# Softmax units before stick-breaking units, and the diff branch's w_o products moved beneath the latter, in a two-layer attention trunk

## The chip, the cores and the metric

The kernel runs on one core of a Trainium2 chip. The metric is the device time of one execution in microseconds, as the median of several runs. The engines are TensorE (PE, matmuls and transposes), VectorE (DVE), ScalarE (ACT), GpSimd (POOL) and SyncE (SP, which issues most of the transfers). TensorE's clock has two levels, 2.4 and 1.2 GHz; the profile gives the granted clock as a share of the higher one.

## What is computed

Two layers run over a sequence of 512 rows of width 1024, in float32. Each is an attention part and a SwiGLU FFN (hidden width 2816); a last RMS norm ends the trunk. Of the attention part:

```python
h = rms_norm(x, g_attn)
proj = h @ w_in            # diff q,k,v; stick-breaking q,k,v; 2 x 1024 gate columns
dq, dk = apply_rope(dq), apply_rope(dk)
w = softmax(dq1 @ dk1) - lam * softmax(dq2 @ dk2)      # 4 diff heads, causal
o_diff = rms_norm(w @ dv, subln) * (1 - lam_init)
log_beta, log_rem = log_sigmoid(z), log_sigmoid(-z)    # z = sq @ sk / 8, 8 stick-breaking heads
a = exp(log_beta + cumsum_from_the_right(log_rem))
o_sb = a @ sv
g_diff, g_sb = split(sigmoid(gates + b_gate))
merged = g_diff * (o_diff @ w_o_diff) + g_sb * (o_sb @ w_o_sb)
x = x + merged @ w_out
```

## The kernel before

Everything lies transposed, features on the 128 partitions and the 512 rows along the free axis. A float32 operand is held as two parts, `hi` (rounded) and `lo` (the rest), and each product of a 128 x 128 tile is three matmuls, `hi.hi`, `lo.hi`, `hi.lo` (`mm_tiles`, L254). A projection to 128 columns from all 1024 features ("a group") is thus 8 x 3 = 24 matmuls of 128x512.

Weights are streamed in the order in which they are used: SP loads a tile into `wr`, ACT rounds it to `wh` (L127), and DVE, or POOL for every fourth tile of `w_in`, makes `wl` = `wr` - `wh` (L128-L129). Four tiles of `wh` and `wl` exist, and a tile is prepared two groups ahead.

PSUM has eight banks: three with the tag `mm` (projections) and five with `at` (scores, transposes, attention products).

In the attention part of a layer, eight units follow one another. Each has three groups (k, q, v) and two maps of scores:
- Four stick-breaking units (SB, names with `s`), first in the order. A map is scores (L465), two sigmoids on ACT (L504, L506), a scan on DVE (L509), a product on POOL (L511), ten transposes (L488) which ACT and DVE copy out as `ths` and `tls` (L491, L492), and a product with v, `avs` (L522, L523).
- Four softmax units (Diff, names with `d`). Their k and q are rotated in `rope` (L400): ACT copies the projection to `us`, POOL multiplies it by the sine table `cs[:,1]` (L405), DVE by the cosine table (L406), four DMAs on SP swap blocks of 32 partitions (L409), and POOL adds (L410). The tables `cs` are multiplied by the norm factor `r` once in each layer (L355, L356). Exponentials stand on ACT (L551), the division by the first map's sums on POOL (L559), the mix of the two maps on DVE (L567). The output is normed per head: three ACT passes over the product `avd` (`ofd`, `osd`, `ohd`, L582 to L587), a mean by PE (`omd`, L589), then logarithm and exponential on ACT (L206, L207) and steps on DVE.

After its k is made (`stack_k`, L428), a unit's casts are `ka`, `kb` on ACT and DVE. The value group (`value`, L447) is first scaled by `r` on DVE (L397), then transposed on PE (`vt`, L450).

The layer's norm factor `r` comes from a matmul (`msa`, L246), logarithm and exponential on ACT and three DVE steps (L205 to L211). Unit 0's three groups are computed ahead of it, on `at` banks; the groups of unit 1 follow.

A loop of 18 steps (L614) puts the work in program order: the first half of map i, groups from a list `slots`, the second half of map i - 2. `slots` names for each unit the groups that stand beside it: the three of the next unit, and gate groups (16 in all), so that the first four units have 3 groups each, the last four 4. Nine gate groups remain for the end. Then come the splitting of the eight outputs into parts (L636), and for each of eight column tiles m of w_o two products, `ws` (stick-breaking half) and `wd` (diff half), whose gates get their sigmoid there (L655) and are multiplied and summed on DVE. ACT holds one table of functions at a time; explicit loads stand at L341 (sigmoids), L623 (logarithm and exponential) and L666. Within these dependences a list scheduler puts each engine's instructions in order when the program is built; each engine runs its list in order and waits where an operand is missing.

Of the kernel before, what the change touches and what calls it, by code (L numbers as in the profile page):

```python
# [8 lines left out]
F32 = mybir.dt.float32  # L9
# [25 lines left out]
BUFS = dict(mx=4, sm=4, blk=12, tmp=5, stk=6, v=3, wk=4, wT=3)  # L35
BANK_BUFS = dict(mm=3, at=5)
W_BUFS, W_AHEAD = 4, 2
GATES_IN_BLK = 4
# [6 lines left out]
FILL = (3, 3, 3, 3, 4, 4, 4, 4)  # L45
# [8 lines left out]
def trunk(ctx: ExitStack, tc, xT, par, tab, scn, msk, w_in, w_o, w_out, w_fi, w_fo, out):  # L54
# [11 lines left out]
    UNITS = [("s", i) for i in range(4)] + [("d", i) for i in range(4)]  # L66
# [5 lines left out]
    GATES = []  # L72
    for m in range(8):
        GATES += [("in", 24 + 8 + m), ("in", 24 + m)]
    layer_order = list(unit_groups(UNITS[0]))
    slots = []
    gi = 0
    for n in range(8):
        g = unit_groups(UNITS[n + 1]) if n < 7 else []
        while len(g) < FILL[n] and gi < len(GATES):  # L80
            g.append(GATES[gi])
            gi += 1
        slots.append(g)
# [18 lines left out]
    def w_src(k):  # L102
        l, kind, i = k[:3]
        if kind == "fo":
            c0, c1 = CHUNKS[k[3]]
            return w_fo[l, i][:, c0 * P:c1 * P]
        return {"in": w_in, "o": w_o, "out": w_out, "fi": w_fi}[kind][l, i]
# [4 lines left out]
    def w_pieces(*steps):  # L112
# [10 lines left out]
        for n_cols in steps:  # L123
# [4 lines left out]
            eng = nc.gpsimd if stream[n][1] == "in" and n % 4 == 0 else nc.vector  # L128
# [199 lines left out]
    for l in range(DEPTH):  # L328
        h = nrm.h
        with ExitStack() as ac:  # L330
# [10 lines left out]
            table("sigmoid_and_others", state["exp"])  # L341
# [4 lines left out]

            def blk(name, dt=F32):
                return T("blk", name, dt=dt)
# [6 lines left out]
            nc.vector.tensor_tensor(out=cs[:, 0], in0=cs[:, 0], in1=r, op=ALU.mult)  # L355
            nc.vector.tensor_tensor(out=cs[:, 1], in0=cs[:, 1], in1=r, op=ALU.mult)  # L356
# [8 lines left out]
            pair = [None]  # L365
            TAIL = list(TAIL0)

            def gate_group(key):
# [3 lines left out]
                n = len(gates)  # L372
                if n < GATES_IN_BLK:
                    t = blk(f"gt{j}")
                elif n < GATES_IN_BLK + BUFS["stk"]:
                    t = T("stk", f"gt{j}")
                elif n < GATES_IN_BLK + BUFS["stk"] + 2:
                    t = T(f"klz0{n - GATES_IN_BLK - BUFS['stk']}", f"gt{j}")
                else:
                    q = (n - GATES_IN_BLK - BUFS["stk"]) % 2  # L380
                    if q == 0:
                        pair[0] = T("wk", f"gt{j}", (P, 1280))
                    t = pair[0][:, q * S:q * S + S]
# [112 lines left out]
            class SB(Unit):  # L496
                def maps(self, c):
# [5 lines left out]
                    for i, (o, n) in enumerate(BANKS):  # L503
                        nc.scalar.activation(out=e[:, o:o + n], in_=bs[i][:, :n], func=AF.Sigmoid, scale=-0.125)  # L504
                    for i, (o, n) in enumerate(BANKS):
                        state["sig"] = nc.scalar.activation(out=z[:, o:o + n], in_=bs[i][:, :n], func=AF.Sigmoid,  # L506
                                                            scale=0.125)

                    nc.vector.tensor_tensor_scan(out=e[:, ::-1], data0=e[:, ::-1], data1=msc[:, ::-1], initial=1.0,  # L509
                                                 op0=ALU.mult, op1=ALU.max)  # L510
# [3 lines left out]
                def mix(self, c, a):  # L514
# [9 lines left out]
                    if c == 0:  # L524
                        self.o = blk("o" + self.n)
# [11 lines left out]
            class Diff(Unit):  # L537
                def maps(self, c):
# [75 lines left out]
            for i in range(16 + LAG):  # L614
# [5 lines left out]
                if i < 16:  # L620
                    units[i // 2].first(i % 2)
                    if i == 7:
                        state["tab"] = table(LNEXP, state["sig"])  # L623
# [281 lines left out]
```

## Time and profile before

| | |
|---|---|
| runs | 1496.0, 1497.68, 1497.97 us (median 1497.68) |
| profiled execution | 1496.57 us, span 1494.8 us, granted clock 0.995 |
| PE busy | 1461.4 us, 98% of the span |
| DVE busy | 976.0 us, 65% |
| ACT busy | 691.8 us, 46% |
| POOL busy | 483.0 us, 32% |
| transfers | 139.73 MB, 93 GB/s on average |

The time of an execution is its span and 1.8 us around it. Busy shares are means over stages: stick-breaking units stand from about 40 to 140 us and 775 to 880 us, softmax units from 140 to 230 and 880 to 970 us, and the rest are gate, w_o, w_out and FFN products. The windows give each engine's busy time stage by stage. The end of a matmul is modelled by the profile, so a pause behind one looks shorter than from start to start.

### The profile page before, as it was taken

What the parts mean: (1) busy time and instruction counts of PE and PEld (TensorE: products, weight loads), DVE (VectorE), ACT (ScalarE), POOL (GpSimd) and SP (SyncE); (2) the same over time, 40 slices, a digit from 0 to 9 for tenths busy, and PEclk for the clock granted to TensorE, in tenths of its full rate; (3) what the DMA queues carried; (4) which work ended last, traced back from release to release, by engine and by line L of the source; (5) the groups of instructions that cost most, each with busy time, mean ns of one, the idle gap of its engine ahead of it and who ended that gap; (6) DMA issues with size and microseconds to landing.
All of it is one profiled execution on the core that took longest, in us unless ns stands there. A gap on an engine that the chain in (4) does not pass through costs nothing.

```text
span 1494.8 us, 19780 instructions
## 1 busy us (share of the span) xinstructions
PE 1461.4 (98%) x7670; PEld 1253.0 (84%) x7670; DVE 976.0 (65%) x1229; ACT 691.8 (46%) x1122; POOL 483.0 (32%) x317
## 2 busy tenths in 40 slices
PE   9899999999999999999998999999999999999996
PEld 7788888888888998998886878888888989989885
DVE  6978776475765757654658777765648467477544
ACT  5656554643642433433444645546336334335342
POOL 2454652001140723530224455510022226155112
PEclk9999999999999999999999999999999999999998
DMA  7122232132323323223421122322323233232232
GB/s 254 46 78 69 75 102 86 57 124 94 106 96 103 108 87 105 90 83 87 134 85 57 64 75 88 100 81 80 103 94 117 90 99 113 74 124 71 87 88 66
DMA packets 45934, 139.73 MB, mean 93 GB/s; under 512 B 5904, under 2 KB 8336, under 8 KB 45840
## 3 DMA queue, kind: packets, MB, share of 16 engines
q1 hardware_dynamic: 45120, 137.91, 28.7%
q8 instruction: 60, 0.98, 0.3%
q10 hardware_dynamic: 720, 0.56, 0.1%
q14 instruction: 34, 0.28, 0.1%
HBM read 132.16 MB, written 2.10 MB: 90 GB/s over the span
## 4 chain that ended last, share of the span: by engine, by line
PE 87%; DVE 6%; ACT 3%; issue 1%; POOL 1%; DMA 1%; SPq 0%; DVEq 0%; POOLq 0%; ACTq 0%
PE fa L725 8%; PE fc L725 4%; PE pg L259 4%; PE pg L260 4%; PE pg L261 4%; PE fo L259 3%; PE fo L260 3%; PE fo L261 3%; PE fg L259 3%; PE fg L260 3%; PE fu L261 3%; PE fg L261 3%; PE fu L260 3%; PE fu L259 3%; PE fb L725 2%; PE wo L259 2%
## 5 line engine op out<-in xcount | busy, mean ns | idle before, releaser
L127 ACT CAST wh<-wr 128x1024 fp32r<-128x1024 f32 (+4 forms) x223 | 213.8, 964 | 327.5 <-issue 55.3
L129 DVE TENSOR_TENSOR wl<-wr,wh 128x1024 fp32r<-128x1024 f32 (+3 forms) x201 | 247.6, 1236 | 77.4 <-ACT wh L127 75.9
L259 PE MATMUL pg<-hha,wh 128*128 128x512 f32 x256 | 101.0, 394 | 0.0
L261 PE MATMUL pg<-hla,wh 128*128 128x512 f32 x256 | 100.3, 392 | 0.0
L260 PE MATMUL pg<-hha,wl 128*128 128x512 f32 x256 | 100.1, 391 | 0.0
L129 POOL TENSOR_TENSOR wl<-wr,wh 128x1024 fp32r<-128x1024 f32 (+3 forms) x22 | 50.7, 2305 | 111.8 <-ACT wh L127 99.2
L706 POOL TENSOR_TENSOR p<-u,g 128x512 f32<-128x512 f32 x22 | 34.4, 1563 | 158.0 <-DVE u L763 154.5
L242 POOL TENSOR_TENSOR accf<-accf,sqf 128x512 f32<-128x512 f32 x10 | 18.5, 1846 | 199.9 <-ACT sqf L240 199.9
L259 PE MATMUL fo<-ah,wh 128*128 128x512 f32 (+1 forms) x220 | 82.8, 376 | 0.0
L260 PE MATMUL fo<-ah,wl 128*128 128x512 f32 (+1 forms) x220 | 82.6, 375 | 0.0
L261 PE MATMUL fo<-al,wh 128*128 128x512 f32 (+1 forms) x220 | 82.3, 376 | 0.0
L259 PE MATMUL pd<-hha,wh 128*128 128x512 f32 x192 | 76.4, 398 | 0.3 <-ACT knd3s L404 0.3
L260 PE MATMUL pd<-hha,wl 128*128 128x512 f32 x192 | 76.2, 397 | 0.0
L261 PE MATMUL pd<-hla,wh 128*128 128x512 f32 x192 | 76.0, 396 | 0.0
L144 POOL TENSOR_TENSOR tf<-ru,rg 128x512 f32<-128x512 f32 x22 | 31.8, 1446 | 128.5 <-DMA ru<-in_w_fi_dram 112.3
L259 PE MATMUL fg<-hhf,wh 128*128 128x512 f32 x176 | 69.1, 393 | 0.0
L260 PE MATMUL fg<-hhf,wl 128*128 128x512 f32 x176 | 69.1, 393 | 0.0
L261 PE MATMUL fu<-hlf,wh 128*128 128x512 f32 x176 | 68.7, 390 | 0.0
L261 PE MATMUL fg<-hlf,wh 128*128 128x512 f32 x176 | 68.7, 390 | 0.0
L260 PE MATMUL fu<-hhf,wl 128*128 128x512 f32 x176 | 68.6, 390 | 0.0
L259 PE MATMUL fu<-hhf,wh 128*128 128x512 f32 x176 | 68.6, 390 | 0.0
L259 PE MATMUL ps<-hha,wh 128*128 128x512 f32 x144 | 58.8, 409 | 0.0
(452 smaller groups left out, 4492.0 us busy)
## 6 DMA issues: line engine op xcount, KB each, us to landing
wr<-in_w_in_dram SPq DMA_DIRECT2D x78, 512.0 KB, 3.3
wr<-in_w_fi_dram SPq DMA_DIRECT2D x44, 512.0 KB, 3.3
wr<-in_w_fo_dram SPq DMA_DIRECT2D x32, 384.0 KB, 3.1
rg<-in_w_fi_dram SPq DMA_DIRECT2D x22, 512.0 KB, 3.3
ru<-in_w_fi_dram SPq DMA_DIRECT2D x22, 512.0 KB, 3.3
wr<-in_w_fo_dram SPq DMA_DIRECT2D x32, 320.0 KB, 2.9
wr<-in_w_o_dram SPq DMA_DIRECT2D x16, 512.0 KB, 3.3
wr<-in_w_out_dram SPq DMA_DIRECT2D x16, 512.0 KB, 3.3
```

The costliest lines, as they stand in the source:

```text
L127: nc.scalar.copy(out=hi[:, c], in_=raw[:, c])
L129: state["wl"] = eng.tensor_tensor(out=lo[:, c], in0=raw[:, c], in1=f32(hi[:, c]), op=ALU.subtract)
L144: tt = lambda eng, o, a, b: eng.tensor_tensor(out=o, in0=a, in1=b, op=ALU.subtract)
L242: eng.tensor_tensor(out=self.acc, in0=self.acc, in1=sq, op=ALU.add)
L259: nc.tensor.matmul(dst, hi[:, c], rh, start=first and k == 0, stop=False)
L260: nc.tensor.matmul(dst, lo[:, c], rh, start=False, stop=False)
L261: nc.tensor.matmul(dst, hi[:, c], rl, start=False, stop=last and k == n - 1)
L706: (nc.vector if u.space == bass.MemoryType.PSUM else nc.gpsimd).tensor_tensor(out=p, in0=u, in1=g, op=ALU.mult)
L725: nc.tensor.matmul(dst, x[:, c], y, start=first and k + n == 0, stop=n == 2 and k == len(a) - 1, skip_group_check=True)
```

## The change

The softmax units come first and the stick-breaking units last. `slots` is written out: one gate group of the diff half beside each of the first three units, two beside the fourth and the fifth, then the last one. w_o is loaded in halves of 512 columns. The diff halves (`od`, 12 matmuls each) become fillers beside the stick-breaking units: each product is multiplied into its gate as soon as it is there (`od_group`); so the diff outputs are split into parts inside `mix`. The stick-breaking halves (`os`) are left for the end, the first two of them with three of their four units early. Five gate groups remain for the end. One load of the sigmoid table stands behind the last softmax unit's exponentials; the gates made so far get their sigmoid there and the later ones as they come; the load of the logarithm's table stands behind the last of them. The loads at the start of a layer and amid the units go. POOL makes no `wl` of a layer's first seven tiles. Gates and outputs get buffers of their own, and the scratch for DMA descriptors is halved. The matmuls are the same in number and size, DMA issues go from 358 to 374 (halves), ACT_TABLE_LOADs from 13 to 9.

```diff
-    UNITS = [("s", i) for i in range(4)] + [("d", i) for i in range(4)]
+    UNITS = [("d", i) for i in range(4)] + [("s", i) for i in range(4)]
...
+    GD, GS = [("in", 24 + m) for m in range(8)], [("in", 32 + m) for m in range(8)]
+    OD = [("od", m) for m in range(8)]
+    slots = [GD[0:1], GD[1:2], GD[2:3], GD[3:5], GD[5:7], GD[7:8] + OD[0:2], OD[2:6], OD[6:8] + GS[0:3]]
+    for n in range(7):
+        slots[n] = unit_groups(UNITS[n + 1]) + slots[n]
+    TAIL0 = GS[3:8]
...
+        if kind in ("od", "os"):
+            return w_o[l, i][:, 512 * (kind == "os"):][:, :512]
...
-            eng = nc.gpsimd if stream[n][1] == "in" and n % 4 == 0 else nc.vector
+            eng = nc.gpsimd if stream[n][1] == "in" and n % 4 == 0 and n % len(layer_order) > 6 else nc.vector
...
             r = nrm.finish()
-            table("sigmoid_and_others", state["exp"])
...
+            def od_group(m):
+                b = bank("mm", f"wd{m}_{l}")
+                hi, lo = w_get(l, "od", m)
+                mm_tiles(b, hi, lo, od_, True, True)
+                nc.vector.tensor_tensor(out=gates[m], in0=b, in1=gates[m], op=ALU.mult)
...
+            def sigmoid(j):
+                bias = pt[:, C_BG + 16 * l + j:C_BG + 16 * l + j + 1]
+                with tc.issue_after(state["tab"].ins):
+                    sigs.append(nc.scalar.activation(out=gates[j], in_=gates[j], func=AF.Sigmoid, bias=bias))
...
+                    od_.append(parts(o, T("osp", "oh" + self.n, dt=F32R), T("osp", "ol" + self.n, dt=F32R)))
...
+                    if i == 8:
+                        fill(g.pop(0))
+                        units[3].second(1)
+                        state["tab"] = table("sigmoid_and_others", state["exp"])
+                        for j in sorted(gates):
+                            sigmoid(j)
                     units[i // 2].first(i % 2)
-                    if i == 7:
-                        state["tab"] = table(LNEXP, state["sig"])
...
-                bs, bd = fbank(f"ws{m}_{l}"), fbank(f"wd{m}_{l}")
-                mm_tiles(bs, hi, lo, os_, True, True, 4)
-                mm_tiles(bd, hi, lo, od_, True, True, 0)
+                if m < 2:
+                    b, hi, lo = ws[m]
+                    mm_tiles(b, hi, lo, os_[3:], False, True, 3)
+                else:
+                    b = fbank(f"ws{m}_{l}")
+                    mm(b, (l, "os", m), os_)
...
-            table(LNEXP, sig)
+            with ExitStack() as order:
+                for s in sigs[:-1]:
+                    order.enter_context(tc.issue_after(s.ins))
+                table(LNEXP, sigs[-1])
```

How the built order of three engines moves. First DVE at the start of layer 0, behind the norm factor `ya0`; `p00` to `p02` are unit 0's k, q and v groups. Before:

```order
L355 TENSOR_TENSOR cs_0_322<-cs_0_322,ya0_311 128x512
L356 TENSOR_TENSOR cs_0_322<-cs_0_322,ya0_311 128x512
L397 TENSOR_TENSOR kns0_0_334<-p00_0_197,ya0_311 128x512
L397 TENSOR_TENSOR qns0_0_344<-p01_0_198,ya0_311 128x512
L397 TENSOR_TENSOR vns0_0_352<-p02_0_199,ya0_311 128x512
L397 TENSOR_TENSOR kns1_0_420<-ps10_0_389,ya0_311 128x512
L397 TENSOR_TENSOR qns1_0_461<-ps11_0_430,ya0_311 128x512
L433 CAST kas0_0_336<-kns0_0_334 64x512
L434 CAST kbs0_0_337<-kns0_0_334 64x512
```

and now:

```order
L206 SCALAR_TENSOR_TENSOR ya0_311<-ta0_312,ya0_311 128x512
L348 TENSOR_TENSOR cs_0_321<-cs_0_321,ya0_311 128x512 x2
L408 TENSOR_TENSOR knd0_0_334<-knd0s_0_335,cs_0_321 128x512
L125 TENSOR_TENSOR wl9_647<-wr9_645,wh9_646 128x1024
L408 TENSOR_TENSOR qnd0_0_353<-qnd0s_0_354,cs_0_321 128x512
L435 CAST kad0_0_344<-knd0_0_334 64x512
L436 CAST kbd0_0_345<-knd0_0_334 64x512
L399 TENSOR_TENSOR vnd0_0_369<-p02_0_199,ya0_311 128x512
L437 TENSOR_TENSOR klz00_0_325<-knd0_0_334,kad0_0_344 64x512
L438 TENSOR_TENSOR klz01_0_326<-knd0_0_334,kbd0_0_345 64x512
L457 TENSOR_TENSOR vd0_0_376<-vtd0_0_371,vd0_0_376 128x512
```

The scaling of the value group, the fifth operation behind the factor before, now stands behind both table products, two cosine products, a weight subtraction and the two casts of the rotated k (`knd0`). On PE the transpose that reads it stands at the same place in both, behind the groups of unit 1.

Second PE at the end of softmax unit 1 in layer 0 (the product is `avd1`, the mean `omd1`, gate group 26 `pg26`, the scores of unit 3 `sd30`). Before:

```order
L260 MATMUL pg26_0_2275<-hha06_161,wl29_2183 128x512
L261 MATMUL pg26_0_2275<-hla06_162,wh29_2182 128x512
L259 MATMUL pg26_0_2275<-hha07_166,wh29_2182 128x512
L260 MATMUL pg26_0_2275<-hha07_166,wl29_2183 128x512
L261 MATMUL pg26_0_2275<-hla07_167,wh29_2182 128x512
L589 MATMUL omd1_0_2100<-ohd1_0_2101,ones_v_79 128x512
L473 MATMUL sd300_0_2148<-kad3_0_1931,qad3_0_1981 128x128
```

and now:

```order
L576 MATMUL avd1_0_1131<-thd1_0_1113,vd1_0_576 128x256
L577 MATMUL avd1_0_1131<-tld1_0_1114,vd1_0_576 128x256
L578 MATMUL avd1_0_1131<-thd1_0_1113,vd1_0_576 128x256
L576 MATMUL avd1_0_1131<-thd1_0_1113,vd1_0_576 128x128
L577 MATMUL avd1_0_1131<-tld1_0_1114,vd1_0_576 128x128
L578 MATMUL avd1_0_1131<-thd1_0_1113,vd1_0_576 128x128
L588 MATMUL omd1_0_1148<-ohd1_0_1149,ones_v_79 128x512
L475 MATMUL sd300_0_1200<-kad3_0_980,qad3_0_1030 128x128
L476 MATMUL sd300_0_1200<-klz10_0_327,qad3_0_1030 128x128
```

Before, a whole gate group of 24 matmuls stands between the product (further up) and the mean; now the mean follows the product's last matmul.

Third ACT at the start of layer 0, where `wh8` is the ninth weight tile, whose other part POOL makes. Before:

```order
L127 CAST wh7_496<-wr7_495 128x1024
L206 ACTIVATE ya0_311<-msa0_309,eps_81 128x512
L207 ACTIVATE ya0_311<-ya0_311 128x512
L268 ACT_TABLE_LOAD
L127 CAST wh8_564<-wr8_563 128x1024
L127 CAST wh9_638<-wr9_637 128x1024
```

and now:

```order
L123 CAST wh7_540<-wr7_539 128x1024
L123 CAST wh8_581<-wr8_580 128x1024
L202 ACTIVATE ya0_311<-msa0_309,eps_81 128x512
L203 ACTIVATE ya0_311<-ya0_311 128x512
L406 COPY qnd0s_0_354<-p01_0_198 128x512
L123 CAST wh9_646<-wr9_645 128x1024
L433 CAST kad0_0_344<-knd0_0_334 64x512
L434 CAST kbd0_0_345<-knd0_0_334 64x512
```

The cast of the ninth tile has moved ahead of the logarithm of the norm, and the table load between is gone.

## Rows read from the trace of the kernel before

**Rows 1.** Windows: us, busy by engine (x instructions), PEclk, DMA share, GB/s.

```profile
40.00:80.00 40.00, 32.84 (x160) 26.85 (x159) 36.99 (x35) 22.65 (x42) 20.49 (x10) 0.96 0.16 53
80.00:140.00 60.00, 58.46 (x318) 49.33 (x317) 46.55 (x48) 38.62 (x72) 32.11 (x16) 1.00 0.22 71
140.00:280.00 140.00, 139.70 (x707) 118.56 (x707) 96.85 (x156) 68.30 (x144) 60.10 (x40) 1.00 0.28 87
...
780.00:820.00 40.00, 32.94 (x161) 26.57 (x160) 31.97 (x23) 20.17 (x41) 21.75 (x9) 0.96 0.13 42
820.00:880.00 60.00, 57.38 (x310) 48.66 (x309) 45.96 (x51) 35.97 (x67) 26.79 (x15) 1.00 0.21 69
```

**Rows 2.** Waits of PE: what for, us in total, times, longest.

```profile
PE avs L523 <- DVE tls L492: 10.0, 7, 3.8
PE vts L450 <- DVE vns L397: 3.1, 1, 3.1
...
PE avs L522 <- ACT ths L491: 1.4, 2, 1.1
```

**Rows 3.** Windows behind the long waits; PEclk is third from the end.

```profile
46.00:48.00 2.00, 2.00 (x6) 1.51 (x6) 1.97 (x2) 1.19 (x3) 1.79 (x2) 0.50 0.00 0
48.00:50.00 2.00, 2.00 (x8) 1.59 (x7) 1.97 (x3) 0.00 (x0) 0.00 (x0) 0.67 0.00 0
...
806.00:808.00 2.00, 1.39 (x7) 1.39 (x8) 1.48 (x3) 0.48 (x1) 0.00 (x0) 0.77 0.80 260
808.00:810.00 2.00, 2.00 (x7) 1.61 (x7) 0.00 (x0) 1.95 (x5) 1.65 (x2) 0.50 0.01 2
```

**Rows 4.** Timeline of PE, layer 1: start us, us, instruction, [idle before <- releaser].

```profile
759.94 0.40 PE L260 MATMUL ps<-hha,wl 128*128 128x512 f32 x1
...
771.97 0.39 PE L259 MATMUL ps<-hha,wh 128*128 128x512 f32 x1
```

**Rows 5.** Timeline of PE, start of layer 0.

```profile
40.86 0.39 PE L261 MATMUL ps<-hla,wh 128*128 128x512 f32 x1
44.34 0.66 PE L450 MATMUL vts<-ident,vns 128*128 128x128 f32 x4 [3.09 <-DVE vns L397]
```

**Rows 6.** Timeline of DVE, start of layer 0.

```profile
39.61 2.87 DVE L356 TENSOR_TENSOR cs<-cs,ya 128x512 f32<-128x512 f32 x1
...
43.60 0.68 DVE L397 TENSOR_TENSOR vns<-p,ya 128x512 f32<-128x512 f32 x1
...
48.18 1.22 DVE L129 TENSOR_TENSOR wl<-wr,wh 128x1024 fp32r<-128x1024 f32 x1
```

**Rows 7.** Timeline of POOL, start of layer 0.

```profile
39.18 2.76 POOL L129 TENSOR_TENSOR wl<-wr,wh 128x1024 fp32r<-128x1024 f32 x1 [12.81 <-ACT wh L127]
```

**Rows 8.** Lines 405, 410, 433, 434: ns min/median/max, first and last start.

```profile
L405 POOL TENSOR_TENSOR knd0u<-knd0s,cs x2: 1315/1524/1732, 106.0 to 846.2; 128x512 f32<-128x512 f32 x2
...
L410 POOL TENSOR_TENSOR knd<-knd,knd0s x2: 1294/1713/2132, 112.0 to 852.0; 128x512 f32<-128x512 f32 x2
...
L433 DVE CAST kad<-knd x8: 420/421/2668, 114.2 to 958.9; 64x512 fp32r<-64x512 f32 x8
...
L434 DVE CAST kbs<-kns x8: 422/423/2565, 46.8 to 822.7; 64x512 fp32r<-64x512 f32 x8
```

**Rows 9.** Timeline of POOL, first rope of layer 1.

```profile
852.04 1.29 POOL L410 TENSOR_TENSOR knd<-knd,knd0s 128x512 f32<-128x512 f32 x1 [4.07 <-DMA knd0s<-knd0u]
```

**Rows 10.** Timeline of POOL, start of layer 1.

```profile
766.60 2.41 POOL L129 TENSOR_TENSOR wl<-wr,wh 128x1024 fp32r<-128x1024 f32 x1 [17.92 <-ACT wh L127]
```

**Rows 11.** Timeline of ACT, end of the first softmax unit of layer 0.

```profile
198.21 0.59 ACT L582 COPY ofd<-avd 128x512 f32<-128x512 f32 x1 [0.81 <-PE avd L578]
...
199.18 0.61 ACT L587 ACTIVATE ohd<-avd 128x512 fp32r<-128x512 f32 x1
```

**Rows 12.** Timeline of ACT, table load at the start of layer 0.

```profile
36.75 1.28 ACT L268 ACT_TABLE_LOAD   x1
38.05 1.05 ACT L127 CAST wh<-wr 128x1024 fp32r<-128x1024 f32 x1
```

More of the change, by code (lines that the diff above doesn't have):

```diff
@@ L44 @@
 H = S // 2
-FILL = (3, 3, 3, 3, 4, 4, 4, 4)
 LAG = 2
@@ L70, in unit_groups @@
         return [("in", c + i) for c in ((4, 0, 8) if kind == "d" else (16, 12, 20))]
-    GATES = []
-    for m in range(8):
-        GATES += [("in", 24 + 8 + m), ("in", 24 + m)]
-    layer_order = list(unit_groups(UNITS[0]))
[L76 to L83, printed above, removed]
+    GD, GS = [("in", 24 + m) for m in range(8)], [("in", 32 + m) for m in range(8)]
[4 more added lines that the diff above has]
+    TAIL0 = GS[3:8]
+    layer_order = list(unit_groups(UNITS[0]))
+    for g in slots + [TAIL0]:
         layer_order += g
-    TAIL0 = GATES[gi:]
-    layer_order += TAIL0
-    layer_order += [("o", m) for m in range(8)] + [("out", m) for m in range(8)]
+    layer_order += [("os", m) for m in range(8)] + [("out", m) for m in range(8)]
     FFN = []
@@ L106, in w_src @@
             return w_fo[l, i][:, c0 * P:c1 * P]
-        return {"in": w_in, "o": w_o, "out": w_out, "fi": w_fi}[kind][l, i]
+        if kind in ("od", "os"):
+            return w_o[l, i][:, 512 * (kind == "os"):][:, :512]
+        return {"in": w_in, "out": w_out, "fi": w_fi}[kind][l, i]
     ready = []
@@ L354, in trunk @@
             nc.sync.dma_start(out=cs, in_=tab)
-            nc.vector.tensor_tensor(out=cs[:, 0], in0=cs[:, 0], in1=r, op=ALU.mult)
-            nc.vector.tensor_tensor(out=cs[:, 1], in0=cs[:, 1], in1=r, op=ALU.mult)
+            for a in range(2):
+                nc.vector.tensor_tensor(out=cs[:, a], in0=cs[:, a], in1=r, op=ALU.mult)
             klz = [[T(f"klz{b}{c}", f"klz{b}{c}", dt=F32R) for c in range(2)] for b in range(2)]
@@ L364, in trunk, with parts @@
             gates = {}
-            pair = [None]
+            sigs = []
+            state.pop("tab", None)
+            os_, od_ = [], []
             TAIL = list(TAIL0)
+            def parts(t, hi, lo):
+                nc.scalar.copy(out=hi, in_=t)
+                nc.vector.tensor_tensor(out=lo, in0=t, in1=f32(hi), op=ALU.subtract)
+                return hi, lo
+            def od_group(m):
[3 more added lines that the diff above has]
+                nc.vector.tensor_tensor(out=gates[m], in0=b, in1=gates[m], op=ALU.mult)
             def gate_group(key):
@@ L502, in maps @@
                     z = T("wk", "z" + name, (P, 1280))
[L503 to L510, printed above, removed]
+                    for t, scale in ((e, -0.125), (z, 0.125)):
+                        for i, (o, n) in enumerate(BANKS):
+                            with tc.issue_after(state["tab"].ins):
+                                nc.scalar.activation(out=t[:, o:o + n], in_=bs[i][:, :n], func=AF.Sigmoid, scale=scale)
+                    state["z"] = nc.vector.tensor_tensor_scan(out=e[:, ::-1], data0=e[:, ::-1], data1=msc[:, ::-1], initial=1.0,
+                                                              op0=ALU.mult, op1=ALU.max)
                     nc.gpsimd.tensor_tensor(out=z[:, 0:1279], in0=z[:, 0:1279], in1=e[:, 1:1280], op=ALU.mult)
@@ L627, in trunk @@
                     fill(key)
-                if i >= LAG:
+                if i >= LAG and i != 9:
                     units[(i - LAG) // 2].second((i - LAG) % 2)
```

62 lines of the change are left out of this document (21 added, 41 removed).

## The prediction

> **What bounds the kernel now.** I read the windows first, since a mean over the span hides the stages. TensorE (PE) is busy all the time outside two places: in the FFN stretches every microsecond is filled, and in the softmax stretch from 140 to 280 it lacks 0.30 us. It lacks 7.16 and 1.54 us in the two windows of the stick-breaking stretch of layer 0 (40 to 140), and 7.06 and 2.62 us in those of layer 1 (780 to 880): 8.70 and 9.68 us [rows 1]. The reader should see there that VectorE (DVE) is busy for 36.99 of 40 us in the worst window while PE has 32.84, and that the DMA share is 0.16 and 0.13, so no transfer is behind it. The list of waits then says who is late: seven waits of the second product of a stick-breaking map (`avs`) for the DVE subtraction `tls`, 10.0 us; one of the first value transpose (`vts`) for its scaling on DVE, 3.1 us; two of `avs` for ACT, 1.4 us [rows 2]. Third come the clock windows: after a long wait the granted clock falls from 1.00 to 0.50, which is the lower of its two levels (1.2 for 2.4 GHz). It stood at 0.50 and 0.67 for two microseconds each in layer 0 and at 0.77 and 0.50 in layer 1 [rows 3]: 2 x 0.50 + 2 x 0.33 = 1.66 us, and 2 x 0.23 + 2 x 0.50 = 1.46 us of lost matmul time.
>
> So about 18 us of 1495 lie in stick-breaking waits, and a change that only moves work, with the same matmuls, can win little more than this.
>
> **Part 1, what goes away.** One projection group is 24 matmuls. Matmul number 2 of the list behind the norm in layer 1 starts at 759.94 and number 55 at 771.97 [rows 4], so a step is 12.03 / 53 = 0.227 us, and a group 5.45 us. Before, each of the four stick-breaking units has three groups (72 matmuls) to cover it. By the new table the first three have 120 (five groups, or four and two halves, or three and four halves) and the last 96: the cover grows by 3 x 10.9 + 5.4 = 38 us a layer, against 8.7 and 9.7 us of idle. The four units filled the 100 us from 40 to 140, 25 us each, and DVE was busy at most 92% of that [rows 1]; with two gates more (0.7 us each, and 1.2 us for the weight's subtraction [rows 6]) it has 23 + 4 us of work in 36, 75%. I therefore take all of 8.70 + 9.68 = 18.38 us as removed, then book new waits one by one below. With it goes the lower clock, 1.66 + 1.46 = 3.1 us. The profile shows 0.39 us for a matmul whose step is 0.227 [rows 5], so a wait behind one looks 0.16 us shorter than it is: ten waits [rows 2] hide 1.6 us. **Removed: 23.1 us.**
>
> **Part 2, the start of layer 0.** PE reaches the first value transpose at the same place of its order as before, behind the projections of unit 1, at 40.86 + 0.23 = 41.1 us; before it stood until 44.34 [rows 5]. What it waits for is now farther back. Before, DVE scaled the value group as the fifth operation behind the norm factor. In the new order the casts of the rotated k stand ahead of it, and these need the whole rope: a POOL product with the sine table, four DMAs that swap rows, and a POOL sum. The sine table is ready when DVE has multiplied it by the norm factor. Before, this product took 2.87 us, where the scaling of a block of the same size takes 0.68 [rows 6], because POOL's weight subtraction of 2.76 us ran beside it from 39.18 [rows 7]. In the new order ACT casts that weight tile ahead of the norm's logarithm (third pair of fences), so the subtraction begins around 36.1 and ends around 38.9; held up by it as that product was, DVE's five steps to the table (three of 0.7, two of 0.6 from start to start) end at 42.0, and not held up at 40.8. I take 42.0. Then 1.3 us of POOL product [rows 8]; 4.07 us from its end to the start of the sum, which covers issue and landing of the four DMAs, and 1.29 us of sum [rows 9]; two casts of 0.42 [rows 8]; 0.68 us of value scaling [rows 6]; and some 0.4 us of handing over: 42.0 + 1.3 + 4.1 + 1.3 + 0.8 + 0.7 + 0.4 = 50.6. **A new wait of 9.5 us**, with a lower end of 8.2. Queued behind it on PE are the gate group and the first softmax scores; SP's queue holds one weight load between the two ropes, which is not needed for 10 us. The clock then falls: between 1.0 (the 0.50 window alone) and 2.7, I take **2.0 us**, a bit over what the 3.2-us wait cost.
>
> **Part 3, the start of layer 1.** Here the same chain has the 72 matmuls behind the norm to hide it. PE reaches the transpose at 771.97 + 18 x 0.227 = 776.1 [rows 4]. POOL has a weight subtraction at 766.60 for 2.41 us ahead of the rope [rows 10]: 769.0 + 1.3 + 4.1 + 1.3 + 0.8 + 0.7 + 0.3 = 777.5. **1.4 us** new; between 0 (the table ready first, and the rope ahead of the subtraction) and 5.
>
> **Part 4, the softmax norm.** ACT makes three passes over the finished product, 198.21 to 199.18 + 0.61 = 199.79, and PE's mean (`omd`) needs the third [rows 11]. Before, a gate group lies between the product and the mean. In the new order the mean of unit d1 follows straight behind its product (second pair of fences), in both layers: 1.6 us each, **3.2 us**, and 0.3 for d3. None to 4 are the ends: the reorder may leave less than one pass uncovered.
>
> **Part 5, the rest.** Gates, halves of w_o and their sigmoids are the same matmuls; 16 more DMA issues with the same bytes stand on a queue at a share of 0.13 to 0.22 [rows 1]. The table loads go from 13 to 9; one in the profile is 1.28 us, and no PE row waits for one but the 1.4 us of ACT waits already booked: nothing, as matmuls stand ahead of each. If that cover goes, the load and five gate sigmoids (0.6 us each, estimated from the pass of the same size in [rows 11]) stand ahead of the first stick-breaking sigmoids, some 4.3 us, with 32 matmuls (7.3 us) above them. The sums at the end keep five gate groups (27 us) as cover. I leave 0.5 us a layer for stick-breaking waits that survive: **1.0 us**.
>
> **Sum.** Added: 9.5 + 2.0 + 1.4 + 3.2 + 0.3 + 1.0 = 17.4 us. Removed 23.1. Net -5.7: 1496.57 of the profiled run becomes 1490.9; the median of the runs shown, 1497.68, is 1.1 above that run, so I forecast **1492.0 us**.
>
> **The rivals.** About 0.2% (3 us, so 1494.7 to 1500.7) is what a measurement of this kernel tells from no change.
>
> *A, slower: POOL and DVE hold each other up in the start chain.* It is now a chain of POOL and DVE in turn, while both also have weight subtractions. The rows show how such an operation stretches: the rope's product 1.31 to 1.73 us, its sum 1.29 to 2.13, the two casts 0.42 to 2.67 and 2.56 [rows 8]. That is 0.42 + 0.84 + 2.25 + 2.14 = 5.65 us a layer, twice, and the clock in layer 1 (1.5): 12.8 us, 1504.8. It decides from 8.7 us on. For it: every one of these rows is seen. Against: by the order no POOL operation is due in the chain while the casts run. The Trainium skill's GPSIMD Engine Reference, Specifications, says that POOL shares its SBUF interfaces with VectorE and contends with instructions with two SBUF inputs. By that rule the collisions come whenever the two overlap; the stretched rows agree. Chance 0.15.
>
> *B, no change: a third of the stick-breaking waits stay,* since DVE is late by its own chain (scan, POOL product, transposes, subtraction), whatever PE does beneath. A third of 18.4 - 3.1 + 1.6 us is 5.6, with one lower-clock stretch 7.1: 1499.1. For it: the longest wait was 3.8 us [rows 2]. Against: 38 us of new cover. Chance 0.16.
>
> *C, faster: the start of layer 0 is short.* If the chain overlaps more than I reckon (half, 4.7 us) and the clock holds (2.0): 1485.3. Against: four DMAs and two POOL operations stand in a row. Chance 0.15.
>
> *D, faster: table loads are on the path.* ACT's load of 36.75 took 1.28 us and the next instruction started at 38.05 [rows 12]. Four loads fewer are 5.1 us, of which 1.3 are in the sum already: 1488.2. Chance 0.06. The Trainium skill's ScalarE: Activation LUTs, What ACT_TABLE_LOAD costs, adds a drain of about 1.38 us, 2.66 us for each switch; by that estimate the four loads would give 10.6 us, less the 1.3, and 1482.7. The row speaks against the drain behind a load: 0.02 us lie between it and the next instruction.
>
> **How the numbers follow.** The forecast has the remaining 0.48; its own range, from the ends of parts 2 to 4, is 1486 to 1497. Of it 0.38 lies below 1494.7 and 0.10 within. C and D are faster (0.21). B is 0.11 same and 0.05 slower by its upper half. A is 0.02 same and 0.13 slower. Faster 0.59, same 0.23, slower 0.18. The range 1483 to 1502 leaves out the upper half of A and the far tail of C.
>
> **What would show it.** In the profile after: the longest PE wait should be the first value transpose `vtd0` of layer 0, for `vnd`, 8 to 10 us from 41; the clock at 0.5 behind it; a wait of about 1.5 us at 776 and two for `ohd`; hardly any for `tls`. Windows of the softmax units should be filled as before. I am wrong if `tls` still leads the list (B), if the start waits exceed 13 us and 5 us (A), or if waits appear behind the table load.

## The result: 1.6% slower, and the profile after

| | before | changed |
|---|---|---|
| median of four runs, us | 1497.63 | 1521.19 (1521.07 to 1522.43) |
| ratio | | 1.0159, 95% interval 1.0145 to 1.0174 |
| span of the profiled run, us | 1494.8 | 1520.6 |
| PE busy, us | 1461.4 | 1471.3 |
| granted clock, mean | 0.995 | 0.985 |

The forecast was 1492, its range 1483 to 1502. The span grew by 25.8 us: PE's idle time by 15.9 (from 33.4 to 49.3) and its busy time by 9.9, with the same matmuls. First the windows of the changed kernel (columns as in [rows 1]):

```profile
40.00:80.00 40.00, 28.36 (x128) 23.37 (x127) 25.48 (x40) 16.43 (x34) 25.36 (x18) 0.83 0.26 76
80.00:140.00 60.00, 59.48 (x296) 50.10 (x295) 46.07 (x71) 30.16 (x65) 33.91 (x22) 1.00 0.30 89
140.00:200.00 60.00, 55.18 (x261) 45.80 (x261) 35.20 (x59) 27.25 (x54) 10.37 (x7) 0.91 0.19 61
200.00:240.00 40.00, 37.73 (x190) 30.81 (x189) 34.07 (x31) 29.12 (x55) 21.51 (x9) 1.00 0.16 53
240.00:300.00 60.00, 59.18 (x307) 49.99 (x306) 46.35 (x49) 31.09 (x59) 17.42 (x8) 1.00 0.25 80
...
760.00:800.00 40.00, 37.18 (x157) 29.94 (x156) 19.20 (x23) 13.93 (x20) 13.26 (x11) 0.96 0.38 122
...
840.00:900.00 60.00, 50.42 (x232) 41.22 (x231) 44.24 (x66) 29.67 (x65) 23.12 (x17) 0.93 0.25 80
...
960.00:1000.00 40.00, 38.05 (x200) 31.61 (x200) 33.95 (x32) 22.41 (x44) 15.33 (x7) 1.00 0.16 53
```

In layer 0 PE lacks 11.64 and 0.52 us at the start, 4.82 between the softmax units and 3.09 in the stick-breaking stretch from 200 to 300. In layer 1 it lacks 2.82 at the start, 9.58 in the softmax stretch from 840 to 900, and 1.95 from 960 to 1000. So the stick-breaking stretches, which lacked 8.70 and 9.68 us [rows 1] (3.1 of them at the start of layer 0 [rows 2]), now lack 3.09 and 1.95: that part of the change works. The softmax stretch, where before 0.30 us was missing, has become the place of the waits. The list of PE's waits in the changed kernel says which (columns as in [rows 2]; "issue" stands for a wait that the view cannot assign):

```profile
PE vtd L452 <- issue: 12.1, 2, 10.5
PE pg L255 <- DVE kns L399: 5.7, 2, 2.9
PE omd L588 <- ACT ohd L586: 3.6, 3, 1.7
PE avs L524 <- DVE tls L494: 3.0, 4, 1.2
PE avd L577 <- DVE tld L494: 2.4, 2, 1.9
PE pg L255 <- ACT knd1s L406: 2.3, 2, 1.2
PE vtd L452 <- DVE vnd L399: 1.7, 1, 1.7
PE ts L490 <- DVE vs L463: 1.6, 2, 1.3
...
PE pg L255 <- ACT knd3s L406: 0.9, 1, 0.9
PE td L490 <- DVE vd L457: 0.6, 1, 0.6
```

Two of these lines are in the forecast, the first transpose `vtd` and the mean `omd`; of the stick-breaking waits `avs` and `ts` it has 1.0 us. The three lines of `pg` are not in it: this group waits for DVE's scaling `kns` or ACT's copies `knd1s`, `knd3s`, although it reads none of them. They are the readers of an earlier product, and only when they are done is one of the three `mm` banks free. Nor are `avd`, `td` and the second line of `vtd`.

The clock windows (columns as in [rows 3]) give nearly all of the growth in busy time:

```profile
52.00:56.00 4.00, 2.84 (x9) 1.97 (x8) 1.98 (x3) 2.89 (x5) 3.22 (x3) 0.50 0.02 5
56.00:60.00 4.00, 4.00 (x13) 3.20 (x12) 0.29 (x1) 0.00 (x0) 3.85 (x4) 0.64 0.27 66
...
148.00:152.00 4.00, 3.63 (x9) 2.86 (x10) 3.89 (x9) 3.31 (x8) 1.29 (x1) 0.50 0.00 0
152.00:156.00 4.00, 4.00 (x14) 3.17 (x13) 2.81 (x4) 0.62 (x1) 4.00 (x4) 0.69 0.00 0
...
796.00:800.00 4.00, 3.86 (x10) 3.12 (x11) 3.46 (x3) 1.92 (x4) 3.92 (x3) 0.57 0.27 80
...
852.00:856.00 4.00, 4.00 (x14) 3.14 (x13) 0.69 (x1) 0.52 (x2) 0.00 (x0) 0.72 0.42 131
...
892.00:896.00 4.00, 2.75 (x10) 2.04 (x8) 1.99 (x5) 1.14 (x2) 0.00 (x0) 0.60 0.10 42
...
900.00:904.00 4.00, 4.00 (x15) 3.17 (x14) 3.85 (x6) 1.25 (x3) 4.00 (x3) 0.75 0.00 0
```

Busy time multiplied by what the clock lacks is 1.4 + 1.4 + 1.8 + 1.2 + 1.7 + 1.1 + 1.1 + 1.0 = 10.7 us in these eight rows. Over all windows of 4 us it is 12.6 us (among them 0.7 from 144 to 148, 0.4 each from 848 to 852 and from 896 to 900, 0.3 from 48 to 52); the kernel before has 3.0 by the same windows. The difference, 9.6 us, is nearly the whole growth in busy time (9.9). Each of the rows shown follows one of the waits listed.

The start of layer 0 in the timelines of PE, DVE and POOL (answering [rows 5 to 7] and [rows 9]):

```profile
40.58 0.39 PE L257 MATMUL pd<-hla,wh 128*128 128x512 f32 x1
51.44 1.09 PE L452 MATMUL vtd<-ident,vnd 128*128 128x128 f32 x4 [10.47 <-issue]
53.69 0.80 PE L255 MATMUL pg<-hha,wh 128*128 128x512 f32 x1 [1.16 <-ACT knd1s L406]
```

```profile
37.02 1.80 DVE L204 SCALAR_TENSOR_TENSOR ta<-ya 128x512 f32<-128x512 f32 x1 [5.47 <-ACT ya L203]
...
40.79 1.29 DVE L348 TENSOR_TENSOR cs<-cs,ya 128x512 f32<-128x512 f32 x2 [0.52 <-DVE ya L206]
...
49.76 0.42 DVE L435 CAST kad<-knd 64x512 fp32r<-64x512 f32 x1 [1.15 <-POOL knd L412]
...
50.65 0.69 DVE L399 TENSOR_TENSOR vnd<-p,ya 128x512 f32<-128x512 f32 x1
```

```profile
42.17 1.64 POOL L407 TENSOR_TENSOR knd0u<-knd0s,cs 128x512 f32<-128x512 f32 x1 [3.89 <-DVE cs L348]
...
47.95 1.77 POOL L412 TENSOR_TENSOR knd<-knd,knd0s 128x512 f32<-128x512 f32 x1 [1.95 <-DMA knd0s<-knd0u]
```

The chain runs as the prediction drew it: tables done at 42.1, product 1.64, sum at 47.95 for 1.77, casts, value scaling at 50.65, transpose at 51.44, where 50.6 was forecast. What was not seen stands in the third line of PE: behind the transpose it waits 1.16 us more for a bank, and then runs at the lower clock for some 5 us (the first two clock rows).

The end of unit d1, PE and DVE:

```profile
140.53 0.27 PE L578 MATMUL avd<-thd,vd 128*128 128x128 f32 x1
142.51 0.50 PE L588 MATMUL omd<-ohd,ones_v 128*128 128x512 f32 x1 [1.71 <-ACT ohd L586]
...
144.75 0.73 PE L589 MATMUL omd<-old,ones_v 128*128 128x512 f32 x1
148.37 0.80 PE L255 MATMUL pg<-hha,wh 128*128 128x512 f32 x1 [2.88 <-DVE kns L399]
```

```profile
145.51 0.17 DVE L548 TENSOR_SCALAR mxd<-mxd 128x4 f32<-128x4 f32 x1
147.02 0.69 DVE L204 SCALAR_TENSOR_TENSOR tod<-yod 128x512 f32<-128x512 f32 x1 [1.34 <-ACT yod L203]
147.63 0.68 DVE L399 TENSOR_TENSOR kns<-ps,ya 128x512 f32<-128x512 f32 x1
```

The mean comes 1.71 us late, as forecast. But PE then stands again for 2.88 us: its next group needs the bank of the first stick-breaking unit's k (`ps00`), done long since. DVE, which frees it by the scaling `kns`, has nothing to do from 145.7 to 147.0: `kns` stands in its order behind `tod`, the norm's first step, which waits for ACT's logarithm and exponential of the mean that PE has just made. PE waits for DVE, DVE for ACT, ACT for PE.

### The profile page after: what moved, and what is told of

It is laid out like the page before. It is cut to its first block, busy times and chain, and to the rows that moved or that the text cites. A ratio compares the mean times of both kernels' runs of the same rounds, so it can differ in the third digit from the quotient of the medians.

```text
span 1520.6 us, 19865 instructions
## 1 busy us (share of the span) xinstructions
PE 1471.3 (97%) x7670; PEld 1259.3 (83%) x7670; DVE 982.1 (65%) x1249; ACT 687.7 (45%) x1134; POOL 470.9 (31%) x313
## 5 line engine op out<-in xcount | busy, mean ns | idle before, releaser
L123 ACT CAST wh<-wr 128x1024 fp32r<-128x1024 f32 (+4 forms) x239 | 216.9, 913 | 356.1 <-issue 93.2
L125 DVE TENSOR_TENSOR wl<-wr,wh 128x1024 fp32r<-128x1024 f32 (+4 forms) x221 | 264.7, 1201 | 89.3 <-ACT wh L123 87.7
L255 PE MATMUL pg<-hha,wh 128*128 128x512 f32 x256 | 104.9, 410 | 8.9 <-DVE kns L399 5.7
L256 PE MATMUL pg<-hha,wl 128*128 128x512 f32 x256 | 104.1, 406 | 0.0
L512 POOL TENSOR_TENSOR zs<-zs,es 128x1279 f32<-128x1279 f32 x16 | 40.8, 2552 | 138.7 <-DVE es L510 109.1
L125 POOL TENSOR_TENSOR wl<-wr,wh 128x1024 fp32r<-128x1024 f32 x18 | 44.9, 2492 | 107.0 <-ACT wh L123 80.4
L255 PE MATMUL ps<-hha,wh 128*128 128x512 f32 x192 | 75.9, 396 | 0.3 <-DVE qns L399 0.3
L257 PE MATMUL ps<-hla,wh 128*128 128x512 f32 x192 | 75.7, 394 | 0.0
L256 PE MATMUL ps<-hha,wl 128*128 128x512 f32 x192 | 75.6, 394 | 0.0
L255 PEld LDWEIGHTS pg<-hha,wh 128*128 128x128 f32 x256 | 50.3, 196 | 21.1 <-DVE kns L399 6.7
```

The source lines that it names most:

```text
L123: nc.scalar.copy(out=hi[:, c], in_=raw[:, c])
L125: state["wl"] = eng.tensor_tensor(out=lo[:, c], in0=raw[:, c], in1=f32(hi[:, c]), op=ALU.subtract)
L255: nc.tensor.matmul(dst, hi[:, c], rh, start=first and k == 0, stop=False)
L256: nc.tensor.matmul(dst, lo[:, c], rh, start=False, stop=False)
L257: nc.tensor.matmul(dst, hi[:, c], rl, start=False, stop=last and k == n - 1)
L512: nc.gpsimd.tensor_tensor(out=z[:, 0:1279], in0=z[:, 0:1279], in1=e[:, 1:1280], op=ALU.mult)
```

## The experiments

Fourteen kernels were run, each beside the kernel before on the same chip (whose median was 1497.44 to 1498.15 us there). Ratios are to it; what a variant of the changed kernel gains in us is counted from 1521.19. Theory R, formed from these timelines: the scratch tiles `tmp` form a ring of five buffers, handed out in program order. A norm takes six of them, a rope three; whatever comes later in the program cannot get its buffer, and so cannot release its PSUM bank, ahead of them. Theory C: POOL and DVE hold each other up (the prediction's rival A).

**e1_s0_ring.** Buffers alone:

```diff
 def scaled(self, b, name):
-    t = tmp(name)
+    t = T("os", name) if self.n == "s0" else tmp(name)
```

> The changed kernel, but the scaled k, q and v of the first stick-breaking unit lie in the two buffers that the outputs use later (ring os) and no more in the ring of five scratch buffers (tmp) behind those of the softmax norm of unit d1. Theory R (the ring and the PSUM banks): this frees the k bank early, so the gate groups can follow the product and cover the mean; the waits of 1.9 us for the mean and 3.4 us for the bank, and the lower clock behind them, go in both layers: some 8 us in layer 0 and 6 in layer 1, 1521 to about 1507 us. Theory C (POOL and DVE hold each other up, DVE has too much to do): the ring does not matter, the waits come elsewhere, within 3 us of 1521.

Measured 1512.12 us, 1.0089 (1.0074 to 1.0104): 9 us better than the changed kernel, not 14. The order now puts the group behind the product and the mean behind the group, and no line of `omd` is left in the waits. The windows of the changed kernel and of this one around the mean of d1:

```profile
140.00:160.00 20.00, 15.41 (x63) 12.43 (x63) 14.01 (x22) 9.57 (x21) 7.98 (x6) 0.74 0.15 50
880.00:900.00 20.00, 15.28 (x72) 12.84 (x73) 13.79 (x23) 10.43 (x22) 2.25 (x3) 0.88 0.16 53
```

```profile
140.00:160.00 20.00, 17.50 (x88) 14.58 (x87) 15.90 (x22) 8.39 (x17) 5.32 (x3) 1.00 0.30 101
880.00:900.00 20.00, 19.96 (x98) 16.56 (x97) 15.96 (x23) 8.47 (x17) 2.92 (x2) 1.00 0.24 79
```

PE lacks 4.59 and 4.72 us in the first, 2.50 and 0.04 in the second, and the clock is whole. What is left of the first window is a new wait of 2.5 us, of the product `avd` for DVE: part of the gain was handed to the next in line. The profiled span is 10.7 us shorter, 6.3 of it in PE's busy time, where the lower clock now takes 6.4 us over all windows instead of 12.6, and 4.4 in idle time. This execution had lost 3.3 us ahead of the place that the edit changes: ACT waited 2.6 us for the first transfer of x (0.5 in the changed kernel), and the first transpose starts at 54.74.

**e2_d0_ring.** All scratch tiles of unit d0 (seven) taken from the ring `osp` of eight, as in the diff above with `"d0"` and `"osp"`, in `rope` too.

> The changed kernel, but all scratch tiles of the first softmax unit (rope of k and q, scaled v) lie in the ring of eight (osp) that holds the diff outputs later. Theory R: the second unit's copies then find scratch buffers at once and free the PSUM banks, and PE has 31 matmuls (7 us) to do before the first value transpose; the start wait of layer 0 falls from 10.6 to about 3 us, the 1.5 us behind it and most of the lower clock go: 8 to 11 us in layer 0, 2 to 3 in layer 1, so 1507 to 1511 us. Theory C: the rope chain itself is what is slow, and the gain is under 3 us.

Measured 1511.66 us, 1.0094 (1.0077 to 1.0111), 9.5 us better, 0.7 above theory R's range. PE's timeline at the start of layer 0:

```profile
47.58 0.60 PE L455 MATMUL vtd<-ident,vnd 128*128 128x128 f32 x4
...
61.78 0.50 PE L255 MATMUL pd<-hha,wh 128*128 128x512 f32 x1 [0.99 <-DVE vnd L402]
...
70.80 0.58 PE L478 MATMUL sd<-kbd,qbd 128*128 128x256 f32 x1 [2.37 <-ACT pd L554]
```

The transpose has no wait (it stands behind 31 matmuls for which the changed kernel had no bank); 3.4 us come back at 61.8 and 70.8, the latter for the exponentials, which hold the score banks.

**e3_v0_ring.** The same for the scaled v of d0 alone.

> The changed kernel, but only the scaled v of the first softmax unit leaves the scratch ring. By the order its scaling then comes ahead of the rope on DVE. Theory R: the transpose comes at 43 to 44, but the next group on PE needs a bank which an ACT copy frees, and that copy still stands behind the casts of the rotated k; the wait moves from the transpose to the gate group, until about 51, and the time stays within 3 us of 1521. Theory V (the prediction's reading: PE stands because the value scaling is behind the casts): the start wait of layer 0 falls from 10.6 to about 3 us with the clock, 8 to 11 us less: 1510 to 1513 us.

Measured 1518.07 us (1514.98 to 1523.13), 1.0136 (1.0114 to 1.0158). PE:

```profile
43.94 0.63 PE L452 MATMUL vtd<-ident,vnd 128*128 128x128 f32 x4 [1.82 <-issue]
53.04 0.79 PE L255 MATMUL pg<-hha,wh 128*128 128x512 f32 x1 [8.47 <-ACT knd1s L406]
```

The transpose comes 7.5 us earlier, and the group behind it waits 8.47 us until 53.04, where the changed kernel had it at 53.69. So PE was held by the bank as well, until nearly the same time, and the order of DVE, on which the prediction rested, only decided the name of the wait. The median is 3.1 us below the changed kernel's, just beyond theory R's 3 us, and far from theory V's 8 to 11; its runs spread over 8 us, and the profiled one is the slowest.

**e5_both_rings.** Both edits.

> The changed kernel with both earlier edits: the first softmax unit's scratch in the ring of eight, the first stick-breaking unit's scaled blocks in the output ring. Theory R: the two gains (9.1 and 9.5 us) stand in different places and add: 1521.2 - 18.6 = 1502.6, between 1500 and 1506 us; what then stays above the kernel before are softmax waits for ACT and DVE and the rest of the stick-breaking waits. Rival M: each wait only moves on to the next round trip of PE, ACT and DVE, and the sum is worth no more than one of them: over 1508 us.

Measured 1504.58 us, 1.0044 (1.0029 to 1.0059): 16.6 of 18.6 us add up. Giving two early users their own rings returns 16.6 of the 23.6 us that the change lost. The rest stays with four waits of scores for exponentials (5.7 us in all), four of `avd` (4.4 us) and single ones.

**e4_order_only.** The kernel before with the order of units, the mirrored number of fillers and one sigmoid table; w_o and the gates at the end as before.

> The kernel before with softmax units first, gate groups mirrored (four groups beside each softmax unit, three beside each stick-breaking one), w_o whole at the end, one sigmoid table load behind the last softmax unit. Theory R: the start costs what it costs in the changed kernel (some 14 us and 4 us with the clock, against 5 and none), and the stick-breaking waits of before (some 18 us with the clock, start left out) stay since their cover does not grow: 1515 to 1530 us. Theory F (the moved w_o halves and gates cost the time, not the order of units): 1500 us or less.

Measured 1530.96 us, 1.0222 (1.0206 to 1.0237). The waits:

```profile
PE vtd L449 <- DVE vnd L396: 12.1, 2, 11.4
PE sd L472 <- ACT pd L548: 8.4, 6, 2.4
```

That is 1 us above theory R's range and 31 above theory F's. The order of units, with its one table load, costs 33 us, and the rest of the change (moved gates and w_o halves, the POOL rule, the buffers) gives back 10. The loss is the order's.

**e6_pool_off_start** (the bound 6 of the POOL rule raised to 15) and **e7_tables_back** (two table loads added behind the norm in each layer).

> The changed kernel, but POOL makes no weight subtraction for the first 16 tiles of a layer (7 before); DVE makes the two. Theory R: collisions at the start cost what the rows show beyond their plain durations, 1.1 us of DVE's first step of the norm factor and about 1 us in the rope: at most 2 us in each layer, 1517 to 1521 us. Theory C (rival A of the prediction): POOL and DVE holding each other up is the main part of the slow start; 5 to 10 us less, 1511 to 1516 us.

> The changed kernel with two table loads more at the start of each layer, behind the norm's exponential (sigmoids, then logarithm and exponential again): 13 loads in all, as before the change. Theory R: ACT is idle there for 3.5 us while the rope waits for the factor, nothing on PE waits for them: within 2 us of 1521. Rival D: loads are on the path, 4 x 1.28 = 5.1 us more, 1526, or up to 10.6 more with a drain on each.

Measured 1522.76 us, 1.0163 (1.0148 to 1.0178), and 1521.32 us, 1.0155 (1.0140 to 1.0170). Neither moved the time beyond its interval; the first missed both of its ranges (1.8 us above R's, 6.8 above C's). Collisions lengthen single rows: DVE's first step at 37.02 took 1.80 us while POOL subtracted from 35.88 for 2.40, and 0.69 in e6_pool_off_start, where POOL does not. There PE waits 8.9 us for the first transpose, not 10.5; the time did not follow. So the collisions exist, but they are not the main part of the loss. Four more loads, at a place where ACT was idle, cost nothing. Theory C falls as the main cause, and of rival D's gain by fewer loads nothing shows.

**e8_sb_first_fill.** In the kernel before:

```diff
-FILL = (3, 3, 3, 3, 4, 4, 4, 4)
+FILL = (4, 4, 4, 4, 3, 3, 3, 3)
```

> The kernel before in its own order of units (stick-breaking first); only the gate groups are moved: four groups beside each stick-breaking unit (one gate more), three beside each softmax unit, three gates beside the last. No ring, no table and no w_o product changes. Theory R: the cover of a stick-breaking unit grows by 24 matmuls (5.4 us) without the round trips of a start with softmax; of the 18 us of stick-breaking waits and lower clock about half goes, and the softmax units lose a cover that they hardly need: 1485 to 1494 us. Rival B: DVE's own chain sets the stick-breaking stretch, and more cover beneath buys nothing: 1496 to 1502 us.

Measured 1511.47 us, 1.0094 (1.0077 to 1.0110). Both sides missed. Three windows of it:

```profile
80.00:140.00 60.00, 59.28 (x315) 50.50 (x315) 44.80 (x43) 32.50 (x61) 24.12 (x13) 1.00 0.22 75
...
200.00:240.00 40.00, 35.60 (x184) 29.91 (x183) 23.47 (x43) 22.50 (x52) 19.90 (x16) 1.00 0.24 79
...
940.00:1000.00 60.00, 57.32 (x280) 47.86 (x279) 38.30 (x62) 28.03 (x57) 27.89 (x18) 0.97 0.28 92
```

The stick-breaking window from 80 gains 0.82 us on [rows 1]; the softmax stretches, which had hardly a wait, lack 4.40 and 2.68 us. Two more waits, 1.7 and 2.4 us, stand at the first w_o products of layer 1 (at 1051 and 1055), for ACT's splitting of the last outputs. The waits of the stick-breaking units fall only from 18.7 to 13.9 us by the lists of PE's waits. The softmax units seem to have been free of waits thanks to their fourth group; that they "hardly need" it was wrong here.

**e9, e12, e13, e14**: the kernel before with the two table products later in the program (nothing needs them before the first rope).

```diff
-            nc.vector.tensor_tensor(out=cs[:, 0], in0=cs[:, 0], in1=r, op=ALU.mult)
-            nc.vector.tensor_tensor(out=cs[:, 1], in0=cs[:, 1], in1=r, op=ALU.mult)
...
+            for a in range(2):
+                nc.vector.tensor_tensor(out=cs[:, a], in0=cs[:, a], in1=r, op=ALU.mult)
```

> The kernel before with one move: the two products of the cosine and sine tables with the norm factor stand behind unit 0's three scalings (nothing needs the tables until the first rope, some 65 us later). Theory R applied to the kernel before: the first value transpose of layer 0 waits only because DVE does two table products of 0.7 and 2.87 us ahead of its scaling; it then comes at 41 instead of 44.3, without the lower clock behind it, 3.2 + 1.4 to 1.7 us less; layer 1 has no wait there: 1493 us, between 1491 and 1495. Rival: the unit's later chain (casts, scan) sets the pace and the first scores are no earlier: 1496 to 1499 us.

> The kernel before with the two table products moved to the place in the program behind the seventh step of the unit loop; by the order they then stand on DVE beside the first rope, no more in the stretch of layer 0's start. Theory R: e9_factor_before lost its gain because the table products now stood ahead of the scaling that frees unit 1's first bank (3.1 us at 45); with both scalings ahead of them, neither wait is there and the lower clock goes too: 1492 to 1495 us. Rival S (the list scheduler deals the whole order anew after any edit, and the new deal costs a few us elsewhere, whatever the start gains): 1496 to 1505 us, with the start's wait gone and others in other places.

> The same with the table products behind the scalings of units 0 and 1 that free the first two banks, still in layer 0's start. Theory R: no wait at the first value transpose and none for the bank, 1492 to 1495 us; rival S: 1496 to 1505 us.

> The kernel before with the two table products bound behind a scan of the second stick-breaking unit, well ahead of the first rope: e12_factor_latest with the tables whole for every rope, and an order that differs from that one's in 49 places on PE. Theory R: no wait at the first transpose and none for the bank, 1492 to 1495 us as e12_factor_latest. Rival S: even this small new deal is worth as much as the gain, 1490 to 1502 us without a rule, and a gain of 3 to 5 us is luck of the order.

In e12_factor_latest the first rope of each layer takes the tables without the norm factor; instructions and sizes are the same. Measured: e9 1503.40 us, 1.0039 (1.0026 to 1.0051); e12 1493.47 us, 0.9968 (0.9956 to 0.9981); e13 1503.10 us, 1.0037 (1.0023 to 1.0050); e14 1497.09 us, 0.9996 (0.9987 to 1.0005). e9 missed both of its ranges. In it the bank again takes the place of the transpose:

```profile
41.62 0.60 PE L448 MATMUL vts<-ident,vns 128*128 128x128 f32 x4
45.09 0.47 PE L259 MATMUL ps<-hha,wh 128*128 128x512 f32 x1 [2.87 <-DVE kns L395]
```

In e12, e13 and e14 neither wait is there in layer 0, and only e12 gains. The list scheduler deals all later instructions anew after each edit; in e13 waits of the stick-breaking and softmax units that the kernel before does not have (`sd` for `pd` 1.8 us, `avs` for `os` 1.6, `avs` for `tls` 1.8 at 155) took what the start had won. e12 came out by theory R, outside S's range; e13 and e14 came out by rival S, outside R's 1492 to 1495. So rival S is the better account of the four: a local gain of 3 to 5 us is not larger than what a new deal takes or gives elsewhere (-4.3 to +6.0 us in these four).

**e10_busy_wait.** 44 matmuls more in layer 0, ahead of unit 1's projections, their result overwritten.

> The changed kernel with 44 matmuls of 128x512 more in layer 0, 10 us, whose result is overwritten; by the order they stand on PE ahead of unit 1's projections, so that PE works through the time in which it waited for the rope. If the lower clock behind the wait costs what its slow matmuls show (2.2 us in that stretch, and the 1.5 us behind the transpose stays), the time falls by 1 to 4 us to 1517 to 1520 although PE does 10 us more work; if the clock costs nothing, 1520 to 1523; if PE was not waiting but working there, 1531.

Measured 1520.92 us, 1.0162 (1.0146 to 1.0177). Two windows:

```profile
40.00:52.00 12.00, 11.23 (x50) 8.97 (x48) 6.79 (x5) 3.94 (x5) 9.10 (x5) 1.00 0.32 90
52.00:60.00 8.00, 6.69 (x25) 5.61 (x26) 5.97 (x7) 3.25 (x5) 5.33 (x4) 0.79 0.34 98
```

10 us more work on PE cost nothing, so PE was idle there. The time lies in the range recorded for a clock that costs nothing, but the run does not tell what the clock costs: PE still waited for 2 us behind the added work, the clock was 0.79 there, and the wait for `kns` behind the mean of d1 grew from 2.9 to 4.9 us. Over all windows the lower clock took 8.5 us, not 12.6; where that went is not shown beyond this wait.

**e11_one_sb_first.** Order s0, d0 to d3, s1 to s3, with two diff halves beside the last unit but one and six beside the last.

> One stick-breaking unit first, then the four softmax units, then the other three stick-breaking units with the diff halves of w_o beneath them; the table products as in e9_factor_before; 13 table loads; six diff halves beside the last unit, eight gate groups at the end. Theory R: a layer that starts with an unrotated unit has no rope in front of its first products, so the start costs no more than before (1 to 5 us less than in the kernel before), and the later stick-breaking units have the new cover; softmax waits as in e5_both_rings may stay: 1488 to 1500 us. Rival M (the waits of the changed kernel come with any mixed order, since the chains of both kinds are then in flight together): 1505 us or more.

Measured 1531.66 us, 1.0228 (1.0209 to 1.0246). Theory R's figure failed, rival M's held: with a stick-breaking unit in front, the rope's wait comes one unit later (`vtd` for its scaling, 7.9 us). This run also moves the table products and has 13 table loads, so it does not isolate the order. No kernel that computes the whole reference beat the kernel before.

## Why the prediction was wrong

- **Part 1, what goes away.** Idle time in the stick-breaking stretches fell from 15.3 us (start left out) to 5.0. I left 1.0 us for waits that survive; the list has 4.6 (`avs` 3.0, `ts` 1.6). 38 us of cover in each layer did not remove them; that DVE's own chain sets them is likely, not shown.
- **Part 2, the start of layer 0.** The wait was 10.5 us where 9.5 was forecast, by the chain named. Missing was the bank behind it (1.16 us), which by e3_v0_ring holds PE nearly as long when the transpose does not wait: the forecast had one of two causes. The lower clock cost 0.3 + 1.4 + 1.4 us (windows 48 to 60), above the range given (1.0 to 2.7).
- **Part 3, the start of layer 1.** The two lines of the list leave 1.6 us for it (12.1 - 10.5) against 1.4 forecast, again with a bank wait behind (2.3 - 1.16 = 1.1 us) and a lower clock (1.7 us) that were not.
- **Part 4 is the step that failed.** "1.6 us each, 3.2 us, and 0.3 for d3" holds as far as it goes (3.6 us). But I stopped at the mean and did not ask what PE does next. The group behind it waits 2.9 us in each layer for a bank, and with the waits for the mean they bring the clock down: 0.7 + 1.8 + 1.2 us in layer 0 (144 to 156) and 2.6 in layer 1 (888 to 904). Waits for the bank and clock together are 12.0 us that the forecast put at nothing. With e1_s0_ring this place alone is worth 9 us.
- **Part 5, the rest, "nothing"** was wrong for the softmax units, above all of layer 1: `avd` 2.4 (0.5 of it in layer 0), `vtd` 1.7, `knd3s` 0.9 and `td` 0.6 us, and 1.5 us of lower clock from 848 to 856. They have as many fillers as before, and e8_sb_first_fill shows how little those units can spare; why each of these waits came is not shown.
- **The sum.** Of 18.9 us more idle time than forecast (15.9 in place of -3.0), the lines name 1.0 + 2.3 + 5.7 + 5.6 + 3.6 and 0.3 for the first transpose of layer 1 and `omd`: 18.5. Of busy time I forecast 2.7 us less and got 9.9 more, 9.6 of them the clock. By part, waits and clock together miss by 3.6 us (1), 3.3 (2), 3.0 (3), 12.0 (4) and 7.1 (5), 29.0 of the 31.5 us by which the profiled span exceeds the forecast. (The lower end of the forecast's own range, from parts 2 to 4, comes to 1485, not 1486.)
- **The signs.** The longest wait (10.5 us, 8 to 10 were told), the clock behind it, the wait at the start of layer 1 (1.66 us, at 794) and the two for `ohd` came, and none of the signs of being wrong appeared. The one that failed was that the windows of the softmax units would be filled: they lack 4.82 and 9.58 us.
- **The rivals.** A fell as the main cause with e6_pool_off_start, where 1.5 us of it shows at the first transpose. B was right on the stick-breaking waits (a third stayed, 5.0 of 15.3 us) and saw none of the loss. C was the wrong sign. D fell with e7_tables_back: four loads more moved the time by 0.1 us. None of the four rivals was a bank. The Trainium skill's ScalarE: Activation LUTs, What ACT_TABLE_LOAD costs, adds a drain to each switch, 2.66 us in all. The trace does not agree: in e7_tables_back two loads in a row took 2.57 us from 38.13, and ACT's next instruction started at 40.71. Loads at other places were not added.

## What to carry to other kernels

When an order is read for a new wait, go on past it: ask what the waiting engine does next, which PSUM bank or buffer that needs, and behind what its last reader stands. A ring of scratch buffers handed out in program order ties things that share no data; giving one early user a ring of its own was worth 9 us, twice. And where a list scheduler deals the order, an edit's local gain has to exceed what the new deal shifts elsewhere, here some 3 to 6 us either way.

## What was not expected of the hardware

The granted clock was at its lower level behind the wait of 10.5 us until about 58.6 us (0.64 in the window from 56 to 60), and from about 144 to 154.5 us behind and around two waits of 1.7 and 2.9 us in a row. Busy time multiplied by what the clock lacks is 3.1 us in the first place (48 to 60) and 3.8 us in the second (144 to 156): a short pair of waits cost as much clock as the long one. Ten microseconds of PE work put into a wait cost nothing (e10_busy_wait).
